# Where a kernel's opening stage makes its sums: raw differences kept in place, third weights and additions moved ahead

## The chip, the core and the metric

The kernel runs on one core of a Trainium2 chip. The metric is the time of one execution on the device in microseconds; before the change it was 1722.41 us, the median of three runs (1721.44 to 1725.9).

The core has five engines that work at the same time, each through its own instructions in order: PE (TensorE, the matmuls, with its weight loads shown apart as PEld), DVE (VectorE), ACT (ScalarE), POOL (GpSimd) and SP (SyncE, which here only issues transfers). They wait for each other through semaphores. Matmuls accumulate in PSUM, in banks of 128x512 float32; all else lies in SBUF.

## The reference, cut to what matters

One layer of a decoder trunk, on 2048 rows x of 1024 columns:

```python
mod = jax.nn.silu(c) @ w_ada[l] + b_ada[l]
shift, scale, gate = jnp.split(mod, 3, axis=-1)
u = x * (1.0 + scale[:, None, :]) + shift[:, None, :]
h = u @ w_in[l]
q, k, v, a_gate, p_in, p_gate, m_a, m_p = jnp.split(h, offsets, axis=-1)
a = sliding_window_sink_attention(q, k, v, sinks[l], bias, mask) * jax.nn.silu(a_gate)
a = a @ w_attn_proj[l]
p = jnp.einsum('bsgc,gcd->bsgd', multiscale_causal_pool(p_in), w_pool_mix[l]).reshape(B, S, POOL_WIDTH)
p = (p * pool_scale[l]) * jax.nn.silu(p_gate)
p = p @ w_pool_proj[l]
y = jax.nn.sigmoid(m_a) * a + jax.nn.sigmoid(m_p) * p
y = (y @ w_out[l]) * (1.0 + gate[:, None, :])
x = layer_norm(DEEPNORM_ALPHA * x + y, ln_gain[l], ln_bias[l])
```

The change touches only the beginning: the modulation, u for the first 1024 rows, and the first columns of u @ w_in (the attention gates).

## The kernel before, in words

Every large product is made from blocks by a scheme of seven block products in place of eight. For a quad (two weight tiles of 128 output columns by two halves of the rows) the activations come as seven sets, B11, T1, T2, B21, T3, B22 and T4, each with four parts (`sets`, 128x512 per part). The T sets are sums and differences of blocks: T1 = B12 - B11, T2 = B22 - T1, T3 = T2 - B11 (in the tile of B11), T4 = B21 - T2 (in the tile of B21). The weights of a quad (`Quad`, line 244) get their own sums: `sum1` (L268) when they arrive, `mid` (L272, L273), then `late` (L277). float32 is made of two fp32r pieces: ACT copies the high part and DVE subtracts it from the source for the low part (`low`, L131; `pair_split` L303, `half_split` L309, `split_set` L185). A block product has 12 matmuls of 128x512: for each of four parts high by high, high by low, low by high (`product`, line 316). The four weight buffers `w_set` are used in turn: a pair takes two, a half split one.

`head` (line 1166) makes the modulation and the first sets. It goes over eight tiles k of x: `load` brings w_ada's rows and the two halves of x's tile; `pe_modulation` makes the shift with matmuls of one column, `modulation` the scale on DVE; `difference` makes the raw difference of the two halves of x for k < 4 in the place of w_ada's first rows (`ws[0]`); `modulate_x` modulates both halves on ACT; `middle` and `closing` split the parts of B11 or B21 and of T1 or T2. `rest_sums(i)` makes T3 in the tile of B11 and T4 in the tile of B21. All this is written out in order (`Ordered` keeps it so), while what is issued through nc.vector, nc.scalar or nc.sync is placed by a scheduler when the kernel is built. Two quads (the attention gates of four weight tiles) are opened in the head, with B11, T1, T2 and B21 multiplied in pieces between the tiles.

After the head, `back` (line 342) ends the two opened quads: additions of u2 and p5 (copies of products) in PSUM, then for each quad the split of its third pair of weights, T3 and B22, and then T4 for both. Each result goes to `consume`: a gate is sigmoid on ACT, a product on DVE (L572) and a store. Then `front` (line 332) opens the next group. `third` also asks for the loads of the next group's weights, whose buffer it frees. The parts of B22 and T4 are split in hooks: `rest` is a list of functions, which `first_phase` puts at ticks 4 and 6 of the first group (a tick follows each product). Other hooks bring side work: `sums_to` (x's second half: loads, modulation on DVE, sums on POOL, stores), `gate_modulation` (a w_ada load and a product with c on DVE), `fold_parts` (a product of two pool weights on PE).

Pools: tag "c" (512 columns, for x's tiles in the head and for gates) has 5 buffers in this phase, tag "p" (u2 and p5) 2.

Lines of helpers: whatever goes through `Ordered` has line 56 in the profile, so the tiles tell what it is: set_T are T1 to T4, set_B are B11 to B22, head_B, head_T, head_kk, head_vv and head_qs are rooms that the head borrows.

Of the kernel before, what the change touches and what calls it, by code (L numbers as in the profile page):

```python
# [15 lines left out]
ALU = mybir.AluOpType  # L16
# [6 lines left out]
KT = D // P  # L23
# [36 lines left out]
def kernel(  # L60
# [80 lines left out]
    def bank(tag="mm"):  # L141
        return ps.tile([P, CH], F32, tag=tag, bufs={"mm": 4, "lg": 2, "pt": 1, "pv": 1}[tag], name=tag)
# [160 lines left out]
    def pair_split(ph, raw, a=nc.scalar, d=nc.vector):  # L303
        hi, lo = ph.split(), ph.split()
        a.copy(by_two(hi), raw)  # L305
        low(d, by_two(lo), raw, by_two(hi))
        return halves(hi, lo)
# [8 lines left out]
    def product(acc, w, name, first=False, i0=0, i1=4):  # L316
        t = sets[name]
        hi, lo = w
        for i in range(i0, i1):
            cols = slice(i * P, (i + 1) * P)  # L320
            mm3(
                acc,
                hi[:, cols],
                lo[:, cols],
                t[:, i, 0, :],
                t[:, i, 1, :],
                first and i == 0,
                i == 3,
                skip_group_check=True,
            )  # L330

    def front(ph, q, tick):
# [6 lines left out]
        tick()  # L339
        return a, b, None, None  # L340

    def back(ph, grp, opened, nxt, own, tick):
        st = []
        for q in grp:
            if q.ahead:
                q.ahead(ph, 0)
                defer(2, lambda q=q: q.ahead(ph, 1))
        for q, (a, b, c, w, *copy) in zip(grp, opened):
            p5 = ph.p("p5")
            if w is None:  # L350
                c = bank("lg")
                nc.scalar.copy(c, a)
                nc.scalar.copy(p5, b)
                w = pair_split(ph, q.second())[::-1]
                q.late()
                product(c, w[1], "T2")
            else:
                u2 = copy[0] if copy else ph.p("u2")
                if not copy:
                    nc.scalar.copy(u2, a)  # L360
                if c is None:
                    c = bank("lg")
                    product(c, w[1], "T2", True)
                nc.vector.tensor_tensor(c, c, u2, ALU.add)
                nc.scalar.copy(p5, b)
            tick()
            nc.vector.tensor_tensor(b, c, p5, ALU.add)
            if not copy:
                product(a, w[0], "B21")
            tick()  # L370
            q.consume(ph, 0, 0, a)
            st.append((q, b, c, p5))
        w = {}

        def ask(q):

            defer(1, lambda: q.load(ph, own, nc.sync, None))
            defer(3, lambda: q.sum1(nc.gpsimd))

        def third(x):  # L380
            w[x] = pair_split(ph, st[x][0].third())[::-1]
            if x < len(nxt):
                ask(nxt[x])

        def with_t3(x):
            q, b, c, p5 = st[x]
            product(c, w[x][1], "T3")
            tick()
            nc.vector.tensor_tensor(p5, c, p5, ALU.add)
            q.consume(ph, 1, 1, p5)  # L390

        def with_b22(x):
            q, b, c, p5 = st[x]
            product(b, w[x][0], "B22")
            tick()
            q.consume(ph, 0, 1, b)

        for x in range(len(st)):
            third(x)
            with_t3(x)  # L400
            with_b22(x)
        for q in nxt[len(st) :]:
            ask(q)
        for q, b, c, p5 in st:
            w = half_split(ph, q.a22)
            product(c, w, "T4")
            tick()
            q.consume(ph, 1, 0, c)
# [757 lines left out]
    def head(ph, plan0):  # L1166
# [24 lines left out]
        def load(k):  # L1191
            for w, m in zip(ws[k], (k, KT + k)):
                sp.dma_start(w, (wadat if m < KT else wada)[m])
            if k in (0, 1, 6, 7):
                t = ph.spare() if k < 2 else late[k - 6]
                xs[k] = cols(t, 0), cols(t, 1)
                sp.dma_start(t, xt[0, k])
                return
            if k < 4:
                xs[k] = [ph.c("x") for h in range(2)]  # L1200
            else:
                xs[k] = [cols(vv_room, 0) if k == 5 else ph.c("x"), ph.last(True)]
            for h, x in enumerate(xs[k]):
                sp.dma_start(x, cols(xt[0, k], h))
# [10 lines left out]
            dve.tensor_tensor(mod[:, k : k + 1], mod[:, k : k + 1], sums[k][:, 0:1], ALU.add)  # L1215

        def modulate_x(k):
            for x in xs[k]:
                act.activation(x, x, AF.Identity, bias=mod[:, k : k + 1], scale=mod[:, KT + k : KT + k + 1])

        def minus(dst, a, b):
# [15 lines left out]

        def difference(k):

            t = ts[k] = cols(ws[0][k // 2], k % 2)  # L1240
            minus(t, xs[k][1], xs[k][0])

        def closing(k):
            if k >= 4:
# [7 lines left out]

        def rest_sums(i):
            minus(xs[i][0], ts[i], xs[i][0])
            minus(xs[4 + i][0], xs[4 + i][0], ts[i])

        groups, fills, post, turn = plan0
# [3 lines left out]
        def products(i):  # L1261
            for w, (a, b, _, _) in zip(starts, opened):
                product(a, w[0], "B11", True, i, i + 1)
                product(b, w[1], "T1", True, i, i + 1)

        for k in range(KT):
            load(k)
            if k < 2:
                grp[k].load(ph, False, sp, None)
# [7 lines left out]
        def second_pair(x):  # L1277
# [2 lines left out]
            o[2:] = bank("lg"), pair_split(ph, grp[x].second(), act, dve)[::-1], u2  # L1280
            act.copy(u2, o[0])

        def more(x, name, i0, i1):
            a, b, c, w, _ = opened[x]
            if name == "T2":
                product(c, w[1], name, True, i0, i1)
            else:
                product(a, w[0], name, False, i0, i1)

        for k in range(2, KT):  # L1290
            opening(k)
            if k < 4:
                difference(k)
            if k == 7:
                second_pair(0)
            closing(k - 2)
            middle(k - 1)
            if k == 2:
                for q in grp:
                    q.sum1(dve)  # L1300
                    starts.append(pair_split(ph, q.first(), act, dve))
            modulate_x(k)
            if k in (3, 4):
                grp[k - 3].mid(dve)
            if 3 <= k < 7:
                products(k - 3)
            if k > 5:
                rest_sums(k - 6)
# [10 lines left out]
            more(x, "B21", 3, 4)  # L1319
        for i in (2, 3):  # L1320
            rest_sums(i)
        late_sets(cp, "B22")
        late_sets(cp, "T3", "T4")
        for i in range(4):
            parts("T3", i, xs[i][0])
        grp[0].late(dve)
        dve.tensor_scalar(nsink, nsink, -1.0, None, ALU.mult)
        rest = [
            lambda name=name, c=c: [parts(name, i, xs[4 + i][c]) for i in range(4)]
            for name, c in (("B22", 1), ("T4", 0))  # L1330
        ]
        return opened, cb, rest

    def turned(hooks, turn, gi):
# [3 lines left out]
    def first_phase(ph, plan0, opened, cb, rest):  # L1338
        groups, fills, _, turn = plan0
        hooks = {}  # L1340

        def at(group, pos, f):
            hooks.setdefault((group, pos), []).append(f)

        for g in range(4):
            steps(hooks, groups, (9, 17, 25, 33)[g], fold_parts(ph, g))
        turned(hooks, lambda i: turn(ph, i), 4)
        for j in range(KT):
            at(j // 2, 3 + 5 * (j % 2), lambda j=j: spread_bias(j))
        for i in range(4):  # L1350
            ks = (i, 4 + i)
            todo = sums_to(
                ph,
                u1_d,
                i,
                lambda x, r, ks=ks: sp.dma_start(x, xt[1, ks[r]]),
                lambda x, r, ks=ks: modulate(x, ks[r]),
            )
            steps(hooks, groups, (5, 18, 31, 47)[i], todo)
        for i in range(8):  # L1360
            steps(hooks, groups, 6 + 4 * i, gate_modulation(ph, 2 * KT + i, cb))
        at(3, 0, lambda: ph.turns.clear())
        at(0, 4, lambda: groups[0][1].late(dve))
        for n, f in zip((4, 6), rest):
            at(0, n, f)
        opened_by = [q for _, _, q in fills[:2]]
        return ring(ph, groups, opened, hooks, opened_by, lambda tick: [front(ph, opened_by[0], tick)])
# [75 lines left out]
            sets[n] = set_tile(pl, n)  # L1443

    plans = [gate_quads(s) for s in range(2)]
    with Pools("g0", spare=2, p=2, c=5) as ph:
        started = head(ph, plans[0])
        kq, k, v = rooms_of("first", F32R)
        rooms["fold"] = kq[:2]
        ph.turns["fold"] = cycle([cols2(k, n) for n in range(2)])  # L1450
        ph.turns["gate"] = cycle([cols2(v, 0)])
        ph.turns["spare"] = cycle([None, None, *(as32(x) for x in kq[2:])])
        opened = first_phase(ph, plans[0], *started)
# [104 lines left out]
```

## Time and profile before

| what | value |
|---|---|
| median of three runs | 1722.41 us (1721.44 to 1725.9) |
| profiled execution, its time | 1724.84 us |
| its span in the profile | 1723.1 us |
| PE busy | 1659.3 us (96%) |
| DVE, POOL, ACT busy | 1283.1, 1001.9, 965.8 us |

A row of the timeline has start, duration, engine, line, operation, tiles written and read, and in brackets the idle time before it and what ended that. Rows of one kind that follow each other are joined (x2, x12). A row of stretches has the length, then busy time and number of instructions of PE, PEld, DVE, ACT and POOL, then the granted share of PE's clock, the share of the transfer engines and GB/s. A row of waits has total, times and the longest, in us. Times are from the start of the span, whose first 90 us hold the head and the first group.

### The profile page before, as it was taken

The numbers are of one execution on the slowest core, as the hardware profiler recorded it, in microseconds if no ns is written. First come the engines' busy times: TensorE is split into PE (matmuls) and PEld (weight loads), VectorE is DVE, ScalarE is ACT, GpSimd is POOL, SyncE is SP. The second block draws the span as 40 slices with busy tenths as digits, with TensorE's granted clock in tenths as the row PEclk, the third lists the DMA queues.
The fourth block names the chain that finished last, engine by engine and source line by source line (L and its number), as shares of the span: only waits on it lengthen the run. The fifth ranks groups of instructions, "written<-read, shape, count | busy, mean of one in ns | idle before, by whom it ended". The sixth has DMA issues, their size and how long they took to land.

```text
span 1723.1 us, 24716 instructions
## 1 busy us (share of the span) xinstructions
PE 1659.3 (96%) x8056; PEld 1389.4 (81%) x8056; DVE 1283.1 (74%) x2288; ACT 965.8 (56%) x2002; POOL 1001.9 (58%) x750
## 2 busy tenths in 40 slices
PE   6899999999999999999999999999999989999996
PEld 5788888888888788887788888888777767778885
DVE  5966665787778768557578777786779886979877
ACT  4644446677677555334567776765645345434452
POOL 2054437686867837863376868595667575523442
PEclk9999999999999999999999999999999999999999
DMA  9388853333433468875533344234988896777442
GB/s 354 126 283 284 220 180 129 117 96 125 142 116 104 129 223 269 299 248 184 197 125 96 113 128 157 83 115 157 339 271 321 301 342 243 292 257 250 159 142 103
DMA packets 188850, 336.79 MB, mean 195 GB/s; under 512 B 18337, under 2 KB 44081, under 8 KB 188721
## 3 DMA queue, kind: packets, MB, share of 16 engines
q1 hardware_dynamic: 185600, 330.96, 56.5%
q10 hardware_dynamic: 3088, 4.23, 1.1%
q8 instruction: 64, 1.05, 0.3%
q14 instruction: 66, 0.53, 0.1%
q0 software_dynamic: 32, 0.02, 0.0%
HBM read 227.96 MB, written 110.33 MB: 196 GB/s over the span
## 4 chain that ended last, share of the span: by engine, by line
PE 44%; DVE 9%; DMA 6%; POOL 5%; issue 4%; ACT 1%; SPq 0%; POOLq 0%; DVEq 0%; ACTq 0%
PE mm L56 29%; PE lg L56 11%; DVE w_set L131 3%; PE pv L56 2%; PE pt L56 2%; DVE set_T L56 1%; POOL nxt L56 1%; POOL w_set L56 1%; DMA set_T<-ain_T 1%; DMA W<-y_d 1%; DVE set_B L56 1%; DVE wide L612 1%; POOL W L56 1%; POOL fin L56 1%; DMA g<-ma_d 1%
## 5 line engine op out<-in xcount | busy, mean ns | idle before, releaser
L56 PE MATMUL mm<-set_B,w_set 128*128 128x512 f32 x2664 | 658.5, 394 | 11.0 <-DVE w_set L131 10.6
L56 PEld LDWEIGHTS mm<-set_B,w_set 128*128 128x128 f32 x2664 | 498.2, 189 | 118.5 <-DVE w_set L131 15.2
L56 PE MATMUL mm<-set_T,w_set 128*128 128x512 f32 x1824 | 456.9, 396 | 4.4 <-POOL w_set L56 1.2
L56 PE MATMUL lg<-set_T,w_set 128*128 128x512 f32 x1728 | 420.5, 393 | 16.4 <-DVE w_set L131 9.0
L56 PEld LDWEIGHTS mm<-set_T,w_set 128*128 128x128 f32 x1824 | 336.8, 189 | 76.9 <-DVE mm L56 5.5
L56 PEld LDWEIGHTS lg<-set_T,w_set 128*128 128x128 f32 x1728 | 324.8, 189 | 90.8 <-DVE w_set L131 13.7
L131 DVE TENSOR_TENSOR w_set<-W,w_set 128x1024 fp32r<-128x1024 f32 x138 | 199.4, 1446 | 153.6 <-ACT w_set L305 143.1
L305 ACT CAST w_set<-W 128x1024 fp32r<-128x1024 f32 x138 | 144.9, 1050 | 258.6 <-PE mm L56 174.2
L56 POOL TENSOR_TENSOR w_set<-W,w_set 128x512 fp32r<-128x512 f32 x132 | 172.1, 1311 | 101.7 <-ACT w_set L56 94.5
L268 POOL TENSOR_TENSOR W<-W,A 128x512 f32<-128x512 f32 x46 | 71.0, 1543 | 252.4 <-ACT w_set L312 58.7
L56 ACT ACTIVATE L<-L,nm 128x257 f32<-128x257 f32 (+1 forms) x256 | 127.1, 498 | 25.8 <-DVE nm L56 20.0
L56 POOL TENSOR_TENSOR W<-W 128x512 f32<-128x512 f32 x82 | 108.4, 1336 | 51.6 <-DVE sm L56 30.3
L56 POOL TENSOR_TENSOR spare<-spare 128x512 f32<-128x512 f32 x68 | 122.4, 1803 | 23.8 <-DMA spare<-pin_B 10.3
L277 POOL TENSOR_TENSOR W<-W 128x512 f32<-128x512 f32 x46 | 69.2, 1504 | 108.8 <-DVE w_set L131 99.7
L56 DVE CUSTOM_DVE_ANT_0 L<-lg,bt,nsink 128x256 f32<-128x256 f32 (+1 forms) x256 | 111.7, 473 | 19.8 <-DMA bt<-e_rep 9.0
L56 ACT CAST w_set<-W 128x512 fp32r<-128x512 f32 (+1 forms) x164 | 100.1, 626 | 37.4 <-POOL W L56 25.8
L56 DVE COPY o<-pv 64x256 f32<-64x256 f32 x128 | 54.3, 424 | 82.3 <-PE pv L56 81.0
L272 POOL TENSOR_TENSOR W<-W 128x512 f32<-128x512 f32 x44 | 72.2, 1645 | 68.7 <-DVE w_set L131 59.7
L56 ACT CAST pth<-pt 128x512 fp32r<-128x512 f32 (+1 forms) x128 | 72.8, 569 | 63.0 <-PE pt L56 62.6
L56 ACT ACTIVATE L<-L,sm 128x256 f32<-128x256 f32 (+1 forms) x128 | 64.3, 503 | 67.9 <-DVE sm L56 67.7
L273 POOL TENSOR_TENSOR W<-W 128x512 f32<-128x512 f32 x44 | 79.3, 1803 | 30.7 <-DMA W<-in_win_dram 27.9
L56 DVE TENSOR_SCALAR L<-L,sm 128x256 f32<-128x256 f32 (+1 forms) x128 | 89.8, 702 | 0.0
(225 smaller groups left out, 2445.2 us busy)
## 6 DMA issues: line engine op xcount, KB each, us to landing
W<-in_win_dram SPq DMA_DIRECT2D x42, 512.0 KB, 5.6
W<-in_win_dram SPq DMA_DIRECT2D x42, 256.0 KB, 4.1
A<-in_win_dram SPq DMA_DIRECT2D x42, 256.0 KB, 4.8
ag_d<-sig SPq DMA_DIRECT2D x32, 256.0 KB, 5.2
pg_d<-sig SPq DMA_DIRECT2D x32, 256.0 KB, 4.8
pg<-pg_d SPq DMA_DIRECT2D x32, 256.0 KB, 3.2
pin_B<-fin SPq DMA_DIRECT2D x32, 256.0 KB, 2.1
ag<-ag_d SPq DMA_DIRECT2D x32, 256.0 KB, 3.0
```

Of the source, the lines that this page charges most:

```text
L56: return lambda *args, **kw: self.tc.keep_in_program_order(op(*args, **kw))
L131: engine.tensor_tensor(dst, src, as32(hi), ALU.subtract)
L268: e.tensor_tensor(self.w[:, 1, :], self.w[:, 2, :], self.a22, ALU.add)
L272: e.tensor_tensor(x[:, 1, :], x[:, 1, :], x[:, 0, :], ALU.subtract)
L273: e.tensor_tensor(x[:, 2, :], x[:, 0, :], x[:, 2, :], ALU.subtract)
L277: e.tensor_tensor(x[:, 3, :], x[:, 3, :], x[:, 1, :], ALU.subtract)
L305: a.copy(by_two(hi), raw)
L612: nc.vector.tensor_tensor(dst, g, dst, ALU.add)
```

## The change

- The raw differences of x stay in the tiles of x's second halves (`ts[k] = xs[k][1]`), and for k < 4 only the first half is modulated. T2 is then made in the same tiles.
- The tiles for k = 2 and 3 are taken in another order (`room`): both first halves, then both second ones.
- T4's subtractions (`last_sums`) leave `rest_sums` and go into hooks: parts 2 and 3 at tick 5, 0 and 1 at tick 6, ahead of T4's parts.
- After T3's parts the head itself ends the opened part of both quads: `late`, the additions (`added`), the copy p5 (`kept`; for the first quad at k = 7), the third weights' split of the first quad (`third`). The second quad's follows B22's parts at tick 4. `back` takes them as they are (`copied`, `ready`).
- Hooks: the first `sums_to` from 5 to 8, the second from 18 to 19, `gate_modulation` two ticks later; the hook with the second quad's `late` goes.
- Buffers: p from 2 to 3, c from 5 to 6.

```diff
-        for q, (a, b, c, w, *copy) in zip(grp, opened):
+        for q, (a, b, c, w, *copied) in zip(grp, opened):
+            if copied:
+                p5 = copied[0]
+                tick()
+                tick()
+                q.consume(ph, 0, 0, a)
+                st.append((q, b, c, p5))
+                continue
...
         def third(x):
-            w[x] = pair_split(ph, st[x][0].third())[::-1]
+            q = st[x][0]
+            w[x] = ready.pop(q) if q in ready else pair_split(ph, q.third())[::-1]
...
             if k < 4:
-                xs[k] = [ph.c("x") for h in range(2)]
+                xs[k] = room[k]
...
-            for x in xs[k]:
+            for x in xs[k][: 1 if k < 4 else 2]:
...
-            t = ts[k] = cols(ws[0][k // 2], k % 2)
-            minus(t, xs[k][1], xs[k][0])
+            ts[k] = xs[k][1]
+            minus(ts[k], xs[k][1], xs[k][0])
...
         def rest_sums(i):
             minus(xs[i][0], ts[i], xs[i][0])
+
+        def last_sums(i):
             minus(xs[4 + i][0], xs[4 + i][0], ts[i])
...
+        def added(x):
+
+            _, b, c, _, u2, p5 = opened[x]
+            dve.tensor_tensor(c, c, u2, ALU.add)
+            dve.tensor_tensor(b, c, p5, ALU.add)
+            opened[x][4:] = [p5]
+
+        def kept(x):
+            opened[x].append(ph.p("p5"))
+            act.copy(opened[x][5], opened[x][1])
+
+        def third(x):
+            ready[grp[x]] = pair_split(ph, grp[x].third())[::-1]
...
                 second_pair(0)
+                kept(0)
...
         grp[0].late(dve)
+        added(0)
+        third(0)
+        grp[1].late(dve)
+        kept(1)
+        added(1)
         dve.tensor_scalar(nsink, nsink, -1.0, None, ALU.mult)
-        rest = [
-            lambda name=name, c=c: [parts(name, i, xs[4 + i][c]) for i in range(4)]
-            for name, c in (("B22", 1), ("T4", 0))
-        ]
+
+        def with_b22():
+            for i in range(4):
+                parts("B22", i, xs[4 + i][1])
+            third(1)
+
+        def with_third():
+            last_sums(2)
+            last_sums(3)
+
+        def with_t4():
+            last_sums(0)
+            last_sums(1)
+            for i in range(4):
+                parts("T4", i, xs[4 + i][0])
+
+        rest = with_b22, with_third, with_t4
...
-            steps(hooks, groups, (5, 18, 31, 47)[i], todo)
+            steps(hooks, groups, (8, 19, 31, 47)[i], todo)
         for i in range(8):
-            steps(hooks, groups, 6 + 4 * i, gate_modulation(ph, 2 * KT + i, cb))
+            steps(hooks, groups, 8 + 4 * i, gate_modulation(ph, 2 * KT + i, cb))
         at(3, 0, lambda: ph.turns.clear())
-        at(0, 4, lambda: groups[0][1].late(dve))
-        for n, f in zip((4, 6), rest):
+        for n, f in zip((4, 5, 6), rest):
...
-    with Pools("g0", spare=2, p=2, c=5) as ph:
+    with Pools("g0", spare=2, p=3, c=6) as ph:
```

In the built kernel PE's instructions keep their order throughout. On the other engines the order differs up to the fourth group of the first phase and is the same from there on.

More of the change, by code (lines that the diff above doesn't have):

```diff
@@ L340, in front @@
         return a, b, None, None
+    ready = {}
     def back(ph, grp, opened, nxt, own, tick):
@@ L357, in back @@
             else:
[L358 to L363, printed above, removed]
+                u2 = ph.p("u2")
+                nc.scalar.copy(u2, a)
+                c = bank("lg")
+                product(c, w[1], "T2", True)
                 nc.vector.tensor_tensor(c, c, u2, ALU.add)
@@ L367, in back @@
             nc.vector.tensor_tensor(b, c, p5, ALU.add)
-            if not copy:
-                product(a, w[0], "B21")
+            product(a, w[0], "B21")
             tick()
@@ L1264, in products @@
                 product(b, w[1], "T1", True, i, i + 1)
+        room = {2: [], 3: []}
+        for h in range(2):
+            for k in room:
+                room[k].append(ph.c("x"))
         for k in range(KT):
@@ L1281, in second_pair @@
             act.copy(u2, o[0])
+        def added(x):
[8 more added lines that the diff above has]
+            ready[grp[x]] = pair_split(ph, grp[x].third())[::-1]
         def more(x, name, i0, i1):
-            a, b, c, w, _ = opened[x]
+            a, b, c, w = opened[x][:4]
             if name == "T2":
@@ L1321, in head @@
             rest_sums(i)
-        late_sets(cp, "B22")
-        late_sets(cp, "T3", "T4")
+        late_sets(cp, "B22", "T3", "T4")
         for i in range(4):
```

## The prediction

> **What bounds the kernel now.** First the page: how long TensorE (PE) stands still in all.
>
> ```profile
> span 1723.1 us, 24716 instructions
> PE 1659.3 (96%) x8056; PEld 1389.4 (81%) x8056; DVE 1283.1 (74%) x2288; ACT 965.8 (56%) x2002; POOL 1001.9 (58%) x750
> ```
>
> PE is idle for 64 us (1723.1 - 1659.3). The change keeps PE's order of instructions, so it can only move such waits (and PE's clock). Next the stretches and the waits of the head and the first groups:
>
> ```profile
> 60.00:80.00 20.00, 15.57 (x62) 12.13 (x61) 18.52 (x29) 11.70 (x20) 2.68 (x2) 0.91 0.50 163
> PE lg L56 <- DVE mm L367: 2.8, 1, 2.8
> PE lg L56 <- DVE w_set L131: 1.6, 1, 1.6
> PE mm L56 <- DVE w_set L131: 0.9, 1, 0.9
> ```
>
> In 60 to 80 us DVE (third pair) is busy 18.5 of 20, PE 15.6. All three waits end on DVE; they sum to 5.3 us. The timeline shows where:
>
> ```profile
> 49.24 1.84 PE L56 MATMUL lg<-ct,head_qs 128*128 128x1 f32 x16
> 51.12 0.15 DVE L56 TENSOR_TENSOR mod<-mod,lg 128x1 f32<-128x1 f32 x1
> 54.80 0.68 DVE L56 TENSOR_TENSOR head_vv<-head_vv,head_B 128x512 f32<-128x512 f32 x1
> 59.17 0.68 DVE L56 TENSOR_TENSOR x<-head_B,x 128x512 f32<-128x512 f32 x1
> 60.98 0.68 DVE L56 TENSOR_TENSOR head_kk<-head_kk,head_B 128x512 f32<-128x512 f32 x1
> 63.92 0.84 PE L56 MATMUL mm<-set_B,w_set 128*128 128x512 f32 x3
> 66.85 0.70 DVE L367 TENSOR_TENSOR mm<-lg,p 128x512 f32<-128x512 f32 x1 [0.30 <-ACT p L365]
> 67.61 0.73 PE L56 MATMUL lg<-set_T,w_set 128*128 128x512 f32 x2 [2.84 <-DVE mm L367]
> 68.66 1.21 DVE L131 TENSOR_TENSOR w_set<-W,w_set 128x1024 fp32r<-128x1024 f32 x1
> 69.93 4.03 PE L56 MATMUL lg<-set_T,w_set 128*128 128x512 f32 x10 [1.58 <-DVE w_set L131]
> 70.39 1.28 DVE L56 TENSOR_TENSOR set_B<-A,set_B 128x512 fp32r<-128x512 f32 x2
> 79.23 2.88 PE L56 MATMUL mm<-set_B,w_set 128*128 128x512 f32 x12
> 81.95 5.64 PE L56 MATMUL lg<-set_T,w_set 128*128 128x512 f32 x24
> 82.20 1.04 ACT L305 CAST w_set<-W 128x1024 fp32r<-128x1024 f32 x1
> 87.43 0.61 PE L56 MATMUL mm<-set_B,w_set 128*128 128x512 f32 x2
> 88.97 2.56 PE L56 MATMUL mm<-set_B,w_set 128*128 128x512 f32 x10 [0.93 <-DVE w_set L131]
> ```
>
> PE ends B21 at 64.8, gets T3's first quad going only at 69.93, ends B22's second quad at 82.1, both T4 at 87.4, and opens the next group properly at 88.97. After that it has no wait until the attention. So 88.97 is the mark: what the change does to it, it does to the time. Steady, a product of 12 matmuls takes 2.72 (79.23 to 81.95), 0.227 each. A DVE operation on 128x512 takes 0.60 (59.17 and three more to 61.58: 60.98 + 0.60), a 128x1024 one 1.13 to the next start.
>
> **Part by part.** *Removed activations.* Four modulations of the second half of x leave ACT:
>
> ```profile
> 31.54 1.52 ACT L56 ACTIVATE x<-x,mod 128x512 f32<-128x512 f32 x2
> ```
>
> 0.76 each, 3.0 us. None of the waits quoted ends on ACT, and DVE is the busier of the two, so 0; if ACT held DVE anywhere it would be a gain, bounded by the 3.0. The two copies moved to the head (p5) are ACT's too, 0.6 each, and lie in its idle time (11.7 busy of 20 in the row above). The extra buffers cost no instruction; the branch for opened quads in back() only drops the copies and additions that the head has made, and PE's matmuls stay in their places.
>
> *Two subtractions taken from ahead of 59.17.* The first (at 49.10) stands before 51.12, which waits for PE (49.24 + 1.84 = 51.08): 0. The second (54.80) brings DVE forward by 0.60, to 58.57 for x.
>
> *T3's start.* Then come two subtractions (1.2, where four stood), four parts of T3 (2.4, to 62.2), late, the first quad's two additions and a gate product (2.4, to 64.6), the third weights' low part (1.13 + 0.1 tail: 65.8). PE is free at 64.8 and takes T3's third matmul at 65.9 instead of 69.93: 4.0 us sooner. DVE goes on with late, two additions and a gate product of the second quad (68.2), B22's parts (70.7), the second quad's low part (71.8). PE does T3 to 68.2, B22 at the pace of its parts to 71.5, T3 to 74.2, B22 to 77.0, where the trace has 82.1: 5.1 us sooner.
>
> *T4.* Now stands behind that on DVE: p, half weights, gate product, two subtractions, gate product, two subtractions, p, half weights: ten at 0.60, to 77.8; then T4's four parts. ACT's copies for these parts stand behind the next group's first weight copy, which waits for the buffer that B22 frees (82.20, right after 82.1 now; so 77.1 + 1.04 + 0.6 = 78.7). Alone, the parts would run 78.7 to 81.1 (78.7 + 4 x 0.60), T4 (its last two matmuls of the first quad, then 2.72 for the second) would end at 84.3, and the mark come at 84.8: 4.2 sooner. But POOL comes in here:
>
> ```profile
> 77.24 1.54 POOL L268 TENSOR_TENSOR W<-W,A 128x512 f32<-128x512 f32 x1 [58.74 <-ACT w_set L312]
> 78.29 2.74 DVE L56 TENSOR_TENSOR set_T<-head_kk,set_T 128x512 fp32r<-128x512 f32 x2
> 78.86 1.62 POOL L273 TENSOR_TENSOR W<-W 128x512 f32<-128x512 f32 x1
> 86.61 0.68 DVE L572 TENSOR_TENSOR sig<-sig,lg 128x512 f32<-128x512 f32 x1
> 87.21 3.94 DVE L131 TENSOR_TENSOR w_set<-W,w_set 128x1024 fp32r<-128x1024 f32 x2
> 87.91 2.16 POOL L273 TENSOR_TENSOR W<-W 128x512 f32<-128x512 f32 x1
> 113.12 1.29 POOL L268 TENSOR_TENSOR W<-W,A 128x512 f32<-128x512 f32 x1 [6.48 <-DVE mod L56]
> ```
>
> Two DVE operations that should take 1.28 take 2.74 beside POOL, two of 2.3 take 3.94; the one that reads PSUM (sig<-sig,lg) keeps 0.68. So each POOL sum, 1.25 alone (the last row), can hold an SBUF operation of DVE once. Now two fall into T4's parts and two later; with the loads earlier all four fall between 72.5 and 80:
>
> ```profile
> 71.14 0.36 SPq L262 DMA_DIRECT2D A<-in_win_dram  x1
> DMA to landing us min/median/max: 2.6/4.6/5.0
> ```
>
> This load, issued when B22's first part ends, now goes out near 69.0, without the two x loads behind it (those wait on SP until T4's subtractions have read the old tiles, near 81), and lands by 72 to 74 (the second row is its range in a quiet stretch); the second quad's follow at 72 to 77. Bounds 0 and 5.0; I take 4.4, since DVE has nearly only SBUF operations there and one POOL sum can run beside a PSUM one. T4's parts then run 82.2 to 84.6, T4 ends at 87.8 and the mark is 88.3: 0.7 sooner. The next group's weights (gate products 1.2, low part 1.13, done by 87.1) are in time, since the modulation of x and the w_ada product (hooks two and three ticks later) now stand behind them. On POOL the x sums move behind the second step of the next weights; nothing on PE waits for these until the second half of the sequence.
>
> The Trainium skill ("SBUF — State Buffer", Who interferes with whom) says that VectorE with two SBUF inputs and GpSimd exclude each other for a whole instruction and the loser blocks. By that rule the four sums cost 0 to 5.0, and the trace agrees (2.74 for two).
>
> *PE's clock.* PE now stands from 77.0 to about 82, with a single matmul in between. Stretches around the present standstill:
>
> ```profile
> 62.90:66.31 3.41, 1.87 (x9) 1.21 (x7) 3.41 (x7) 1.97 (x4) 0.00 (x0) 1.00 0.00 0
> 66.31:69.72 3.41, 0.73 (x2) 0.30 (x2) 3.11 (x5) 3.07 (x7) 0.00 (x0) 1.00 0.49 175
> 69.72:73.13 3.41, 3.20 (x8) 2.53 (x9) 3.16 (x6) 2.62 (x5) 0.00 (x0) 0.50 0.58 165
> ```
>
> After 3.41 us with 0.73 busy the clock is 0.50 for 3.41 us, and 8 matmuls pass where 15 would (3.41 / 0.227): 1.6 us. After 1.87 busy it stayed whole. Today's slow stretch is partly hidden, since the mark waits for DVE anyway. Then T4 ends last on PE, so it counts: bounds 0 and two stretches, 3.2; I take 2.0. Sum: -0.7 + 2.0 = +1.3.
>
> The Trainium skill ("TensorE: Matmul & The Clock Gate", Part 1) gates the clock after an idle free-running window of about 3.4 us. Read strictly (no work in it), this would often not happen here, since 4.3 us of standstill hold a whole window in about one phase of four ((4.3 - 3.41) / 3.41); the trace gates with 0.73 of work in it.
>
> The profiled execution took 1724.84, the median of the runs is 1722.41; against the first the sum gives 1726.1, against the median **1723.7**.
>
> **Rivals.**
> *POOL's sums find gaps* (faster): they fall beside PSUM operations or DVE's waits. For: three PSUM operations and 0.8 us of waiting for ACT lie there. Against: four sums, 5 us. Mark at 84.8, no slow clock: 1722.4 - 4.2 = 1718.2.
> *The clock stays whole.* For: phases differ between runs. Against: the rows above, where 0.73 of work did not keep it whole. Mark at 88.3: 1722.4 - 0.7 = 1721.7. It is what the strict reading of the Trainium skill's section, named above, would mostly give.
> *The fold's weights come late* (slower). SP issues them behind a gate store that waits for DVE's products after T4's parts, near 86, as late as now, and DVE now has x's modulation and w_ada's product between them and T2's weights:
>
> ```profile
> 91.17 1.05 ACT L56 CAST first_qs<-first_kk 128x1024 fp32r<-128x1024 f32 x1 [1.26 <-DMA first_kk<-in_wpt_dram]
> 95.21 2.10 DVE L131 TENSOR_TENSOR w_set<-W,w_set 128x1024 fp32r<-128x1024 f32 x1
> 102.36 2.92 PE L56 MATMUL lg<-set_T,w_set 128*128 128x512 f32 x12
> 85.40 1.27 DVE L56 CUSTOM_DVE_ANT_0 first_vv<-first_vv,cb,mod 128x1024 f32<-128x1024 f32 x1
> L56 DVE TENSOR_SCALAR spare<-spare,mod 128x1024 f32<-128x1024 f32 x2 | 1.6, 800 | 0.0
> ```
>
> From landing to T2's weights it takes 6.1 us (91.17 to 97.31), then 9.0 (+ 1.27 + 1.6). T2 needs them near 104.1 (102.36 + 0.45 + 1.3). So it decides from a landing after 95.1, 3 us later than I expect (92 to 93); landing at 97.3 costs 2.2, a slow stretch 1.6 more: +5.1, 1727.5.
>
> **How the numbers follow.** Forecast (0 to +2.7, 1722.4 to 1725.1 as its own range) 0.50; clock whole 0.17; gaps 0.18; fold late 0.10; something else 0.05. A measurement of this kernel tells about 0.3%, 5.2 us, from no change; the runs themselves spread 4.5. Faster by more: a third of "gaps" and some of the rest, 0.08. Slower: most of "fold late", a little of the forecast, 0.11. Same: 0.81. The range runs from "gaps" to "fold late", 1718.2 to 1727.6.
>
> **What would show it.** Right: T3's first quad near 66, B22 ended near 77, PE then waiting some 5 us for set_T on DVE; DVE's subtractions and T4 parts at 1.2 to 1.8 us beside POOL's L268 and L273 rows; clock 0.50 near 80 to 86; the mark near 90. Wrong: T4's parts at 0.6 each (gaps), PE waiting after 100 us (fold), or a T3 start after 67, which would mean the chain on DVE was not the one I followed.

## The result, and the profile after

On one chip the changed kernel took 1727.33 us (median of 22 runs, 1722.18 to 1730.58), the kernel before 1723.44 us (22 runs, 1719.6 to 1727.08). The ratio is 1.0018, with a 95% interval of 1.0011 to 1.0026: by the ratio 3.1 us slower (1.9 to 4.5; the two medians are 3.9 apart), inside the 0.3% that count as no change. The forecast was +1.3 us.

The page of the changed kernel gives the span and PE's busy time; the second fence has PE's four longest waits between 60 and 262 us (three more are of 0.3 each):

```profile
span 1726.6 us, 24719 instructions
PE 1660.6 (96%) x8056; PEld 1388.8 (80%) x8056; DVE 1282.2 (74%) x2288; ACT 962.5 (56%) x1998; POOL 998.1 (58%) x750
```

```profile
PE lg L56 <- DVE set_T L56: 2.6, 1, 2.6
PE lg L56 <- ACT set_T L56: 1.9, 1, 1.9
PE mm L56 <- DVE w_set L131: 1.3, 1, 1.3
PE pv L56 <- DVE first_qs L56: 0.4, 1, 0.4
```

The waits of 2.8 and 1.6 us ahead of T3 have shrunk to 0.3 each, and the wait of 0.9 at 88.97 is gone. In their place PE waits 1.9 and 2.6 us for T4's parts (set_T). The other two rows lie at 187 and 183 us, where the kernel before has no wait. The changed kernel's timeline shows PE from the end of the head on:

```profile
56.84 2.20 PE L56 MATMUL mm<-set_B,w_set 128*128 128x512 f32 x9
...
64.44 2.56 PE L56 MATMUL lg<-set_T,w_set 128*128 128x512 f32 x10 [0.33 <-DVE w_set L131]
...
72.88 2.88 PE L56 MATMUL mm<-set_B,w_set 128*128 128x512 f32 x12
77.71 0.69 PE L56 MATMUL lg<-set_T,w_set 128*128 128x512 f32 x1 [1.94 <-ACT set_T L56]
81.03 7.20 PE L56 MATMUL lg<-set_T,w_set 128*128 128x512 f32 x23 [2.63 <-DVE set_T L56]
88.06 1.30 PE L56 MATMUL mm<-set_B,w_set 128*128 128x512 f32 x5
...
187.44 2.60 PE L56 MATMUL mm<-set_B,w_set 128*128 128x512 f32 x10 [1.29 <-DVE w_set L131]
192.60 2.88 PE L56 MATMUL mm<-set_B,w_set 128*128 128x512 f32 x12
```

```profile
58.48 2.20 PE L56 MATMUL mm<-set_B,w_set 128*128 128x512 f32 x9
190.46 2.88 PE L56 MATMUL mm<-set_B,w_set 128*128 128x512 f32 x12
```

The last fence is the kernel before: the same two groups of matmuls as the first and the last row of the fence ahead of it. PE's order is the same in both kernels, so the start of the same matmul in two traces can be compared directly. The changed kernel is 1.64 us ahead at 58 us (56.84 - 58.48) and 2.14 behind at 190. The mark (third matmul of the next group, 88.97 before) is at 88.06 + 2 x 0.227 = 88.51, 0.46 ahead. The lead at 58 us is not the change's: PE's clock was slow in the head in one profile and whole in the other (last section), and two later kernels with the changed head whose profiles have the same slow stretch, fill and no_sums, stand at +0.12 and -0.18 there. So the change costs 1.2 us up to the mark (-0.46 + 1.64) and 2.6 more between the mark and 190. The experiments below are read by the same differences to the profile before; from 190 to 260 they stay as they are.

The table gives them in us, each row from one profile; "up to the mark" is the change of the lead from 61 us to 88.97, "after it" from there to 260.

| kernel | at 61 | at the mark | at 260 | up to the mark | after it | ratio of times (95%) |
|---|---|---|---|---|---|---|
| changed kernel | -1.64 | -0.46 | +2.14 | +1.2 | +2.6 | 1.0018 (1.0011 to 1.0026) |
| gate_back | -1.44 | -0.22 | -0.24 | +1.2 | 0.0 | 1.0011 (0.9998 to 1.0024) |
| gate_only | -0.61 | -1.03 | -1.31 | -0.4 | -0.3 | 1.0001 (0.9985 to 1.0016) |
| sums2_back | -1.30 | +0.02 | +0.72 | +1.3 | +0.7 | 1.0000 (0.9988 to 1.0011) |
| fill | +0.12 | -0.48 | +1.34 | -0.6 | +1.8 | 0.9994 (0.9983 to 1.0006) |
| no_sums | -0.18 | -2.33 | 0.00 | -2.2 | +2.3 | 0.9995 (0.9985 to 1.0005) |
| t4_first | -2.41 | -6.09 | -2.29 | -3.7 | +3.8 | 0.9993 (0.9979 to 1.0008) |
| t4_first_gate | +0.28 | -4.08 | -1.95 | -4.4 | +2.1 | 0.9988 (0.9973 to 1.0004) |
| t4_first_g18 | -1.29 | -5.46 | -4.24 | -4.2 | +1.2 | 0.9977 (0.9968 to 0.9985) |

**The part up to the mark.** DVE, POOL and ACT of the changed kernel while PE waits for T4 (x2 are two joined):

```profile
72.31 3.49 DVE L56 TENSOR_TENSOR head_kk<-head_kk,x 128x512 f32<-128x512 f32 x2
78.13 1.17 DVE L131 TENSOR_TENSOR w_set<-A,w_set 128x512 fp32r<-128x512 f32 x1
79.22 1.75 DVE L56 TENSOR_TENSOR set_T<-x,set_T 128x512 fp32r<-128x512 f32 x1
80.90 0.68 DVE L56 TENSOR_TENSOR set_T<-head_vv,set_T 128x512 fp32r<-128x512 f32 x1
71.76 1.79 POOL L268 TENSOR_TENSOR W<-W,A 128x512 f32<-128x512 f32 x1 [53.39 <-DVE w_set L131]
73.63 1.62 POOL L273 TENSOR_TENSOR W<-W 128x512 f32<-128x512 f32 x1
77.36 1.38 POOL L268 TENSOR_TENSOR W<-W,A 128x512 f32<-128x512 f32 x1 [2.11 <-DMA W<-in_win_dram]
78.83 1.60 POOL L273 TENSOR_TENSOR W<-W 128x512 f32<-128x512 f32 x1
75.71 1.04 ACT L305 CAST w_set<-W 128x1024 fp32r<-128x1024 f32 x1 [3.05 <-PE mm L56]
```

Undisturbed, two such subtractions take 1.28 and one 0.68. Here three rows take 3.49, 1.17 and 1.75 beside POOL's four sums: 2.2 + 0.5 + 1.1 = 3.8 us lost. ACT's copies for T4 stand behind the next group's weight copy (75.71), which waited for PE. And the clock, by stretches of 3.41 us (the changed kernel; PE's busy time is the second number, the granted clock the third from the end):

```profile
74.45:77.86 3.41, 1.47 (x7) 0.90 (x5) 3.41 (x5) 1.87 (x3) 1.30 (x2) 1.00 0.99 358
77.86:81.27 3.41, 0.78 (x2) 0.28 (x3) 3.41 (x4) 2.46 (x5) 2.48 (x2) 0.50 0.98 320
81.27:84.69 3.42, 3.42 (x9) 2.65 (x10) 3.42 (x6) 0.00 (x0) 0.00 (x0) 0.50 0.71 249
```

Two slow stretches in a row; the second one falls on T4's matmuls.

**The part after the mark.** Of the 2.6 us, 2.0 are lost at 183 and 187 us. The other 0.6 go between 136 and 158 us, in hold-ups too short for a row of waits, most of them at and right behind the fold of the group before, whose weights ACT copies at 151.27 (148.40 in the kernel before); gate_back and sums2_back, below, have no such slip. What is late at 183 starts some 21 us earlier. Rows of the changed kernel, then of the kernel before:

```profile
161.59 1.41 SPq L56 DMA_DIRECT2D spare<-in_xt_dram  x2
169.64 0.81 DVE L56 TENSOR_SCALAR spare<-spare,mod 128x1024 f32<-128x1024 f32 x1 [3.61 <-DMA spare<-in_xt_dram]
170.36 0.68 DVE L396 TENSOR_TENSOR p<-lg,p 128x512 f32<-128x512 f32 x1
171.62 0.57 ACT L56 COPY st<-pv 128x512 f32<-128x512 f32 x1
173.94 1.10 SPq L56 DMA_DIRECT2D first_kk<-in_wpt_dram  x1
180.48 1.05 ACT L56 CAST first_qs<-first_kk 128x1024 fp32r<-128x1024 f32 x1 [1.03 <-DMA first_kk<-in_wpt_dram]
182.84 0.50 PE L56 MATMUL pv<-mhi,first_qs 128*128 128x256 f32 x2 [0.35 <-DVE first_qs L56]
```

```profile
160.59 1.31 SPq L56 DMA_DIRECT2D spare<-in_xt_dram  x2
165.74 0.69 DVE L389 TENSOR_TENSOR p<-lg,p 128x512 f32<-128x512 f32 x1
168.63 0.81 DVE L56 TENSOR_SCALAR spare<-spare,mod 128x1024 f32<-128x1024 f32 x1 [2.19 <-DMA spare<-in_xt_dram]
167.20 0.59 ACT L56 COPY st<-pv 128x512 f32<-128x512 f32 x1
170.16 1.42 SPq L56 DMA_DIRECT2D first_kk<-in_wpt_dram  x1
```

In the changed kernel DVE's modulation of x stands ahead of p (in the kernel before behind it) and waits 3.61 us for its load. p comes at 170.36 instead of 165.74; behind p the gate's sigmoid on ACT, behind that the copy of the fold's result (171.62, not 167.20), behind that its store and SP's next loads of fold weights (173.94, not 170.16). ACT waits 1.03 us for these to land, PE waits 0.35 us for the fold, and DVE, which has the fold's weights ahead of the next group's, holds PE for 1.29 us more (187.44).

### The profile page after: what moved, and what is told of

It reads as the page before. It is cut to its first block, busy times and chain, and to the rows that moved or that the text cites. A ratio compares the mean times of both kernels' runs of the same rounds, so it can differ in the third digit from the quotient of the medians.

```text
span 1726.6 us, 24719 instructions
## 1 busy us (share of the span) xinstructions
PE 1660.6 (96%) x8056; PEld 1388.8 (80%) x8056; DVE 1282.2 (74%) x2288; ACT 962.5 (56%) x1998; POOL 998.1 (58%) x750
## 4 chain that ended last, share of the span: by engine, by line
PE 48%; DVE 9%; DMA 4%; issue 3%; POOL 2%; ACT 1%; SPq 0%; POOLq 0%; DVEq 0%; ACTq 0%
PE mm L56 33%; PE lg L56 12%; DVE w_set L131 2%; PE pv L56 2%; PE pt L56 2%; DVE set_T L56 1%; DVE g L617 1%; DMA g<-ma_d 1%; DVE wide L619 1%; DVE set_B L56 1%; POOL w_set L56 1%; DMA y_d<-wide 1%; DMA set_B<-ain_B 0%; DVE o L56 0%; POOL fin L56 0%
## 5 line engine op out<-in xcount | busy, mean ns | idle before, releaser
L56 POOL TENSOR_TENSOR W<-W 128x512 f32<-128x512 f32 x82 | 108.3, 1335 | 51.7 <-DVE sm L56 30.4
L277 POOL TENSOR_TENSOR W<-W 128x512 f32<-128x512 f32 x46 | 69.1, 1502 | 112.8 <-DVE w_set L131 104.1
L272 POOL TENSOR_TENSOR W<-W 128x512 f32<-128x512 f32 x44 | 69.7, 1587 | 69.3 <-DVE w_set L131 59.1
L273 POOL TENSOR_TENSOR W<-W 128x512 f32<-128x512 f32 x44 | 76.1, 1730 | 29.3 <-DMA W<-in_win_dram 26.9
```

Of the source, the lines that this page charges most:

```text
L56: return lambda *args, **kw: self.tc.keep_in_program_order(op(*args, **kw))
L272: e.tensor_tensor(x[:, 1, :], x[:, 1, :], x[:, 0, :], ALU.subtract)
L273: e.tensor_tensor(x[:, 2, :], x[:, 0, :], x[:, 2, :], ALU.subtract)
L277: e.tensor_tensor(x[:, 3, :], x[:, 3, :], x[:, 1, :], ALU.subtract)
```

## The experiments

**gate_back**: do the later hooks of gate_modulation cost the part after the mark?

```diff
-            steps(hooks, groups, 8 + 4 * i, gate_modulation(ph, 2 * KT + i, cb))
+            steps(hooks, groups, 6 + 4 * i, gate_modulation(ph, 2 * KT + i, cb))
```

> The changed kernel with gate_modulation's hooks back at 6 + 4i; all else as changed. Theory L (late fold): in the changed kernel's trace DVE's second modulation of x stands ahead of p<-lg,p and waits 3.61 us for its load; p comes at 170.36 (165.74 before), the fold's result is copied at 171.62 (167.20), SP issues the next fold weights at 173.94 (170.16), and PE waits 0.35 and 1.29 us between 182 and 188: its lead of 0.03 us turns into a lag of 2.1. With the hooks back p stands ahead of that modulation again; no PE wait between 112 and 260 us, and a time 2.1 us under the changed kernel's: near 1725.2, ratio to the kernel before near 1.0010. Theory M (the mark alone): the loss lies at the first group (T4's parts beside POOL's sums, half clock), and what comes later is taken up by slack: same as the changed kernel within 0.5 us, ratio near 1.0018.

The ratio is 1.0011 (0.9998 to 1.0024), which alone doesn't tell L from M. The trace does: p is at 165.98, ahead of the modulation at 169.41, the fold weights' load at 169.87, and the timeline shows no wait of PE between 84 and 260. Up to the mark the loss is the changed kernel's (+1.2), after it 0.0 instead of +2.6. Its timeline:

```profile
165.98 0.67 DVE L396 TENSOR_TENSOR p<-lg,p 128x512 f32<-128x512 f32 x1
169.41 0.81 DVE L56 TENSOR_SCALAR spare<-spare,mod 128x1024 f32<-128x1024 f32 x1 [2.76 <-DMA spare<-in_xt_dram]
169.87 0.49 SPq L56 DMA_DIRECT2D first_kk<-in_wpt_dram  x1
```

**gate_only**: the later hooks of gate_modulation alone, in the kernel before.

```diff
-            steps(hooks, groups, 6 + 4 * i, gate_modulation(ph, 2 * KT + i, cb))
+            steps(hooks, groups, 8 + 4 * i, gate_modulation(ph, 2 * KT + i, cb))
```

> The kernel before with one part of the change alone: gate_modulation's hooks at 8 + 4i. Theory L: the modulation of x then stands ahead of p<-lg,p on DVE in the third group here too, so some 2.1 us are lost between 180 and 190; against it, the product with c (1.27 us) leaves DVE's queue ahead of the weights that the mark waits for (0.93 us of wait there), so +1.2 to +2.1: 1724.6 to 1725.5, ratio 1.0007 to 1.0012. Theory M: only the gain at the mark shows: 0 to -0.9, ratio 0.9995 to 1.0000.

Ratio 1.0001 (0.9985 to 1.0016). The wait of 0.93 at the mark is gone, but only 0.4 us of it is gained. Theory L failed in the other half: the modulation does stand ahead of p, and yet nothing is lost up to 260. The load goes out at 158.11 here, so DVE waits only 1.82 for it and p is at 167.20:

```profile
158.11 1.40 SPq L56 DMA_DIRECT2D spare<-in_xt_dram  x2
166.48 0.81 DVE L56 TENSOR_SCALAR spare<-spare,mod 128x1024 f32<-128x1024 f32 x1 [1.82 <-DMA spare<-in_xt_dram]
167.20 0.69 DVE L389 TENSOR_TENSOR p<-lg,p 128x512 f32<-128x512 f32 x1
```

So here the order on DVE is not enough: the load must be late too. That load is moved by another hook of the change, the second `sums_to`.

**sums2_back**: the changed kernel with that hook back by one tick.

```diff
-            steps(hooks, groups, (8, 19, 31, 47)[i], todo)
+            steps(hooks, groups, (8, 18, 31, 47)[i], todo)
```

> The changed kernel with the second sums_to's hook back from 19 to 18, nothing else. Since gate_only kept its time although x's modulation stood ahead of p there too, theory L2: both hooks are needed, gate_modulation's to put that modulation ahead of p on DVE, this one to issue its load late (161.59 in the changed kernel, 158.11 in gate_only). Here the order on DVE stays, the load goes out about a tick sooner, DVE waits under 2 us for it (3.61), PE's waits of 0.35 and 1.29 between 182 and 188 go or shrink under 0.5, and the time is 1.5 to 2.1 us under the changed kernel: ratio to the kernel before 1.0006 to 1.0010. Rival L3: the load is late for another reason (the weights that moved ahead of it on SP); the waits stay at 1.6, ratio near 1.0018.

Load at 158.97, DVE's wait 1.44, p at 167.88 with the modulation still ahead of it. PE's wait for the fold is gone, the one for the weights is 0.69 (1.29), and after the mark 0.7 us are lost instead of 2.6. The ratio is 1.0000 (0.9988 to 1.0011). L3 fell, since the load does come sooner with this hook, and L2 stands in the main: either hook put back takes away most of the loss. Its sizes were missed: it had put the wait under 0.5 and the ratio at 1.0006 to 1.0010.

```profile
158.97 1.56 SPq L56 DMA_DIRECT2D spare<-in_xt_dram  x2
167.15 0.81 DVE L56 TENSOR_SCALAR spare<-spare,mod 128x1024 f32<-128x1024 f32 x1 [1.44 <-DMA spare<-in_xt_dram]
186.07 2.56 PE L56 MATMUL mm<-set_B,w_set 128*128 128x512 f32 x10 [0.69 <-DVE w_set L131]
```

**fill**: the price of the half clock. Extra matmuls stand where PE waits for T4 in the first group.

```diff
+        if copied:
+            junk = bank("pt")
+            for n in range(20):
+                mm(junk, sets["B22"][:, 0, 0, 0:P], sets["B22"][:, 0, 0, :], start=n == 0, stop=n == 19)
         for q, b, c, p5 in st:
             w = half_split(ph, q.a22)
```

> The changed kernel with 20 extra matmuls of 128x512 on PE between the second quad's B22 and T4 of the first group (4.5 us at the whole clock, into a bank that nothing reads). Theory K (price of the half clock): they keep PE at work from 75.8 to 80.3, the clock stays whole, T4's matmuls from 81.03 take 5.2 us where they took 7.2, and the mark comes at 86.5 instead of 88.5; the time falls 1 to 2 us, less what the fold takes back (the changed kernel's own late waits stay). Rival K0: the slow stretch costs nothing, since the next group's weights come no earlier: mark at 88.0 or later, time the same. Rival K1: the extra matmuls run at half clock themselves, and T4 starts after 82: slower by 1 us or more.

```profile
82.68 5.52 PE L56 MATMUL lg<-set_T,w_set 128*128 128x512 f32 x23 [0.58 <-DVE set_T L56]
```

No slow stretch after 56 us until 275. T4's 23 matmuls take 5.5 us (7.2), though they start at 82.68: this profile's head is 1.76 us later than the changed kernel's (0.12 against -1.64). Up to the mark the kernel now gains 0.6 where the changed one loses 1.2: the half clock costs 1.8. With the head's 1.76 taken off the mark is at 88.49 - 1.76 = 86.7, where K had 86.5; K holds, and K0 and K1 fell. After the mark it loses 1.8, as the late fold has it; the ratio is 0.9994 (0.9983 to 1.0006).

**no_sums**: the price of POOL's sums. The kernel leaves them out and multiplies with the raw blocks of the second group's weights, so its result is not the layer's.

```diff
+        if copied:
+            for q in nxt:
+                q.sum1 = q.mid = lambda e=None: None
+                q.first = lambda q=q: q.w[:, 0:3:2]
+                q.second = lambda q=q: q.w[:, 2:4]
+                q.late = lambda e=nc.gpsimd, q=q: e.tensor_tensor(q.w[:, 3, :], q.w[:, 3, :], q.w[:, 2, :], ALU.subtract)
```

> The changed kernel without the sums that POOL makes of the second group's weights (sum1 and mid of its two quads; their products use the raw blocks in place of the sums, which is the part of the computation left out). Theory S (POOL's sums hold DVE): from 72.3 to 82.8 DVE loses 4.4 us to four of them; without them T4's second matmul comes at 77 to 78 (81.03), no or one slow stretch of the clock follows, the mark lies near 83 to 84.5. Theory O (order): T4's parts wait for ACT and for what stands ahead of them on DVE; T4 starts within 1 us of 81.03. In time, of 4 to 5.5 us at the mark the fold's weights take some back (as in t4_first, whose mark was 5.6 sooner and whose time was some 4 less): S gives 2 to 4 us under the changed kernel, O under 1.

```profile
73.57 1.29 DVE L56 TENSOR_TENSOR head_kk<-head_kk,x 128x512 f32<-128x512 f32 x2
78.51 0.50 PE L56 MATMUL lg<-set_T,w_set 128*128 128x512 f32 x1 [1.47 <-ACT set_T L56]
79.23 7.12 PE L56 MATMUL lg<-set_T,w_set 128*128 128x512 f32 x23 [0.23 <-DVE set_T L56]
```

DVE's row has its undisturbed length. T4's second matmul comes at 79.23; with the head's 1.46 us taken off (-0.18 against -1.64) that is 77.8, 3.3 sooner than in the changed kernel. So S gives T4's start, and O is part of it: PE still waits 1.47 for ACT, whose copy stands behind the next group's weights. One slow stretch (79.67 to 83.09) stays, and the mark comes 3.4 us sooner than in the changed kernel (-2.2 against +1.2), not the 4 and more that S had promised. After the mark 2.3 are lost. Ratio 0.9995 (0.9985 to 1.0005), which by the ratios is 4.0 under the changed kernel: S's 2 to 4, not O's under 1.

**t4_first**: T4's work on DVE and ACT at once behind the second third weights, POOL's sums as they are.

```diff
-        rest = with_b22, with_third, with_t4
+        def t4_first():
+            for i in range(4):
+                last_sums(i)
+            halved[grp[0]] = half_split(ph, grp[0].a22, act, dve)
+            for i in range(4):
+                parts("T4", i, xs[4 + i][0])
+            halved[grp[1]] = half_split(ph, grp[1].a22, act, dve)
+
+        rest = with_b22, t4_first
...
-        for n, f in zip((4, 5, 6), rest):
+        for n, f in zip((4, 4), rest):
```

> The changed kernel with T4's four subtractions, its parts and both half splits of its weights in written order right behind the second quad's third weights (tick 4), ahead of the sigmoid products; POOL's sums, loads and the gate hooks as changed. Theory O (order): T4 is late because DVE takes p, half splits and gate products between, and ACT's copies stand behind the next group's first weight copy; freed of these, T4's first quad can start near 77 (81.03 in the changed kernel), no second slow stretch of the clock follows, the mark comes near 83 to 85 (88.5): 3 to 5.5 us under the changed kernel, 1722 to 1724. Theory S (POOL's sums): whatever stands at 71.8 to 80 on DVE is held by the four sums, 4.4 us in all, so T4's parts end near 80 and the clock still halves: mark near 86.5, 2 us under the changed kernel or less, 1725.5.

T4 starts at 76.91 with all 24 matmuls in one run, no stretch of the head is slow in this profile, and the mark is at 82.89: 3.7 us gained where the changed kernel loses 1.2, so 4.9 between them: theory O, which had said 3 to 5.5. But 3.8 us are given back by 190: PE waits 0.75 at 94.8 for the fold's weights, 0.52 at 131.8 and 0.98 at 183 for weights behind them. By the starts of the matmuls these three places cost 1.3, 0.8 and 1.1; the other 0.6 go near 122 and 154 us, in hold-ups too short for a row. The ratio is 0.9993 (0.9979 to 1.0008).

**t4_first_gate** has gate_back's hooks with it.

> The version before it with gate_modulation's hooks also back at 6 + 4i. If L and O hold, both gains add: 5 to 7.5 us under the changed kernel, 1720 to 1722, ratio to the kernel before 0.998 to 0.999. If S holds in place of O: near 1723.3, ratio 1.000. If M holds in place of L: as t4_first within 0.5.

Mark 4.4 sooner, 2.1 given back (0.34 at 96, 1.38 at 183); ratio 0.9988 (0.9973 to 1.0004), the small end of the gain that L and O together gave (0.998 to 0.999). At 183 p does stand ahead of the modulation (163.06 and 166.75), and PE waits all the same.

**t4_first_g18** has sums2_back's hook besides.

> t4_first_gate with the second sums_to's hook at 18 again. In t4_first_gate PE waited 1.38 us at 183 for weights behind a late fold; if the late x load is the cause (L2), this wait shrinks under 0.5 and the time is 1 us less than that version: ratio to the kernel before 0.998 to 0.9985. If the wait comes from the fold's own loop (result copy, store, load of the next weights), which PE simply reaches sooner, it stays near 1.4, ratio 0.9988.

The load goes out at 155.50 instead of 158.29, and the wait at 183 is gone: the late load was its cause. So once PE comes 3.6 us sooner than in the kernel before, the late load alone is enough. What is left is one wait at the first fold, 0.95 us. The ratio is 0.9977 (0.9968 to 0.9985): 4.0 us faster than the kernel before (2.6 to 5.5), though this too lies within the 0.3%; the changed kernel's interval (1.0011 to 1.0026) is apart from it. Rows of its timeline (PE, DVE, POOL) and the stretch ahead of and into T4:

```profile
77.50 5.72 PE L56 MATMUL lg<-set_T,w_set 128*128 128x512 f32 x24 [1.40 <-DVE p L398]
95.58 0.50 PE L56 MATMUL pv<-mhi,first_qs 128*128 128x256 f32 x2 [0.95 <-DVE first_qs L56]
71.85 1.29 DVE L56 TENSOR_TENSOR head_kk<-head_kk,x 128x512 f32<-128x512 f32 x2
72.52 5.37 POOL L268 TENSOR_TENSOR W<-W,A 128x512 f32<-128x512 f32 x1 [53.92 <-DMA A<-in_win_dram]
```

```profile
74.86:78.27 3.41, 2.01 (x9) 1.37 (x8) 3.09 (x6) 0.35 (x1) 3.33 (x2) 1.00 0.80 240
```

With 2.01 of 3.41 us busy the clock stays whole here and up to 269 us, and DVE's subtractions run at their full pace while POOL's sum takes 5.37 us.

## Why the prediction was right, and where not

- *T3's start, 65.9 instead of 69.93.* Measured 64.44, with the head 1.64 us early: 66.1 on the axis of before. Right.
- *B22 of the second quad ends at 77.0.* Measured 72.88 + 2.72 + 1.64 = 77.2. Right.
- *POOL's four sums cost DVE 4.4.* Measured 3.8. T4's last part ends at 82.78 + 1.64 = 84.4, forecast 84.6. Right in place and nearly in size; the rival that the sums would find gaps fell, and no_sums shows the price by T4's start (3.3 sooner).
- *The half clock costs 2.0.* 1.8 by fill. It was slow for two stretches, as the rows of before (0.73 of 3.41 us busy, then 0.50) had let expect, and the rival that it would stay whole fell: here 1.47 of 3.41 us did not keep it. The Trainium skill ("TensorE: Matmul & The Clock Gate", Part 1) speaks of an idle window; PE's longest wait here was 2.63 us, so no window of 3.41 was idle, and the measurement decides against the strict reading. (The 4.3 us of standstill that the prediction put into that reading have no working in it; the trace has two, of 1.94 and 2.63.)
- *The mark, +1.3.* Measured +1.2, and +1.2 and +1.3 again in gate_back and sums2_back.
- *"After that it has no wait until the attention ... what the change does to it, it does to the time."* This step failed. It held for the kernel before; the change itself made new waits behind the mark, 2.6 us in the profile. They come from what was costed at nothing: the x modulation and w_ada's product were looked at only where they leave DVE's queue in the second group, not where they arrive later. The rival of the late fold weights had the mechanism (fold weights behind a store, DVE's queue ahead of the next group's weights) but at the first fold, near 102 us, and by other causes; there the trace after shows no wait (t4_first and t4_first_g18, whose PE is 6.2 and 5.6 us ahead by then, have one there, 0.75 and 0.95). It came at the third group.

Up to 260 us the profile gives 1.2 + 2.6 = 3.8, the runs 3.1 (1.9 to 4.5). Of the forecast's 1.3 nothing had to be taken back; what it missed makes up the difference to the measured time and some more. The forecast's own range, 0 to +2.7, did not hold the 3.1. The whole range (1718.2 to 1727.6, with 1722.4 + 3.1 = 1725.5 in it) held it because it was drawn out to the late fold, and that is luck in part: that rival stood for another place.

That the two hooks together make the loss after the mark rests on the traces: the changed kernel, fill and no_sums, which have both, lose 1.8 to 2.6 there, and gate_back, gate_only and sums2_back, which have one, -0.3 to +0.7. The times alone do not show it (1.0011 for gate_back lies in the changed kernel's interval).

What stays open: for sums2_back the trace up to 260 gives +2.0 and the times 0.0 (-2.1 to +1.9), for fill +1.2 and -1.0 (-2.9 to +1.0). Behind 260 us single profiles drift by up to 4 us against each other, and slow stretches of the clock in the attention come in some profiles and not in others (one between 269 and 276 us in the profiles of after, fill and t4_first_g18, none there in gate_back and t4_first), so one profile is no measure of the whole time.

## What to carry to other kernels

A step that frees time at one place moves the queue entries of other work, and each of them has to be followed to where it lands, not only to where it leaves: here two hooks moved by one and two ticks put a DVE operation whose load was late ahead of an addition, some 80 us after the place that was meant to gain, and lost twice as much as the place itself. Before pricing a new gap on the critical engine, ask what stands between its inputs and their start in every queue: here putting T4's parts in written order right behind the last work they need was worth 4.9 us at the mark (+1.2 to -3.7), more than taking away the sums beside them (3.4).

Compare two traces by the start of the same instruction on the engine whose order is unchanged. A table of such differences told causes apart that the times, with intervals 3 to 5 us wide, could not.

## What was not expected of the hardware

- *Who is held, DVE or POOL, is not fixed.* In the changed kernel POOL's sums took 1.4 to 1.8 us and DVE's subtractions 1.8 each (0.64 undisturbed). In t4_first_g18 DVE's operations followed each other from 71.85 to 77.95 (0.60 from one start to the next), and one sum on POOL took 5.37 us instead of 1.3. The Trainium skill ("SBUF — State Buffer", Who interferes with whom) says that the order of issue decides who blocks, and its Summary that the second one to issue blocks until the first finishes. That POOL is held shows here; that it was held for several instructions of DVE, also those issued after its own, goes beyond the sentence. It ended at 77.89, 1.2 us after DVE came to the first operation with an input in PSUM (p<-lg,p, 76.67), so it seems to have got in only there. What lets POOL in between two DVE operations at 74 us of the changed kernel, and not here, was not tried.
- *The head of the same program differs between profiles.* PE's clock was slow from about 35.5 to 39 in the profiles of before, fill and no_sums, and whole then in the other seven; the lead at 61 us varies from -2.4 to +0.3. The same stretch before and after:

```profile
35.00:39.00 4.00, 4.00 (x16) 3.32 (x16) 4.00 (x8) 2.99 (x6) 0.00 (x0) 0.57 1.03 409
```

```profile
35.00:39.00 4.00, 4.00 (x25) 3.49 (x24) 4.00 (x9) 2.29 (x5) 0.00 (x0) 1.00 1.03 406
```

PE passes 16 matmuls in one and 25 in the other. A slow stretch there costs about 1.6 us (the changed kernel's lead goes from +0.15 at 35 us to -1.42 at 45), more than the whole effect at the mark, and has nothing to do with the change: fill and no_sums have the changed head.
- *How much work keeps the clock whole is not one share.* A stretch of 3.41 us with 1.73 busy, 62.43 to 65.84 in gate_only, was followed by the whole clock, and one with 1.99, 271.40 to 274.82 in fill, by 0.50. What else decides was not tried.
